# First modulations of a diffusion block: w_ada loaded and multiplied by eighths of the channels instead of quarters

## The chip, the cores and the metric

The kernel runs on one core of a Trainium2 chip. Its time is the device time of one execution in microseconds (us); three executions of the kernel before give a median of 2354.31 us (2351.40 to 2354.86). The engines are named as the profile names them: PE is TensorE (PEld its weight loads), DVE is VectorE, ACT is ScalarE, POOL is GpSimd, and SP issues DMAs (SPq, ACTq and POOLq are the engines' queues for it).

## The reference

One layer of a hybrid diffusion block. x and ctx are 256 tokens of 2048 channels each; everything is fp32.

```python
mod_c = jax.nn.silu(c_ctx) @ w_ada[l][:, :n_mod * D_MODEL] + b_ada[l][:n_mod * D_MODEL]   # n_mod = 2
mods_c = jnp.split(mod_c, n_mod)
... = _token_mixers(_modulate(h_ctx, mods_c[0], mods_c[1]), ...)      # context: states only
mod = jax.nn.silu(c) @ w_ada[l] + b_ada[l]
sh1, sc1, g1, sh2, sc2, g2 = [m[:, None, :] for m in jnp.split(mod, 6, axis=-1)]
y, _ = _token_mixers(_modulate(x, sh1, sc1), ...)                     # x * (1 + sc1) + sh1
x = _layernorm(ALPHA * x + g1 * y, ln1_g[l], ln1_b[l])
x = _layernorm(ALPHA * x + g2 * _sq_relu_mlp(_modulate(x, sh2, sc2), ...), ...)
```

Only the first two modulations (shift sh1 and scale sc1, for x from c and for ctx from c_ctx) concern the change: two vectors of 2048 inputs times the first 4096 columns of w_ada, 33.6 MB, then x and ctx scaled and shifted by them. The token mixers begin with projections u @ w_in; here the keys of the DeltaNet (512 columns) and its gates (32 columns, loaded as 128) stand at the opening.

## The kernel before

Channels are kept as 16 k-tiles of 128 (kt), tokens of x and ctx side by side as 512 columns. A fp32 product is made of three matmuls with operands split into a high and a low part (`split`: hi on ACT by line 138, lo on DVE by line 139); `cm_block` (lines 219 to 221) is such a triple.

The opening runs over quarters q of the channels (lines 368 to 393). For each quarter and each part (0 shift, 1 scale) `load_ada` asks for four raw tiles of w_ada, each 4 k-tiles by 512 columns (1 MB, 2 KB in a row); even calls go to a ring of two (`ring`), odd ones to general pages (`raw`, tag k8, seven buffers shared with xt and others). There are 32 such tiles. Line 380 multiplies a tile: four matmuls, one per k-tile, with the two silu'd conditioning vectors in 32 columns of weights (`cs32`), each into another 32 partitions of the PSUM bank `pmod`. When a part is complete, `mod_columns` copies the rows to SBUF (ACT, line 359), turns and sums them into columns by four small matmuls with `sel` (line 361), and adds the bias (DVE, lines 363 and 365). When shift and scale of a quarter are there, `modulated` transposes a k-tile of x and ctx on PE (line 171), applies scale and shift on ACT (line 352) and splits it into uh and ul. Then `keys` (two k-tiles, 24 matmuls of 512 columns into four banks psk) and `gates_in` (four k-tiles, 12 matmuls into the bank pga) use them. All these are put in the list `later` and taken from it between the tiles of the following quarter; what is left runs behind the last one. Two steps of the Hyena filters (`next(filt)`, line 255 and around) stand in it too.

Behind the opening come colB and colC (small tables: rows loaded by DMAs on ACT's queue into a tile that DVE cleared, line 181, then transposed on PE), the convolutions on the key banks (DVE, lines 521 to 525, cy), and the next projections over the context (`proj_cm_ctx`). Beside all projections run the loads `aw` of the other modulations' columns (line 540, 512 KB each) with a sum on DVE per load (lines 553 and 555); aw, the weights of projections and the gates' weights share four buffers of the tag wraw.

PSUM has eight banks: four of tag mm (at first psk) and four of tag ps (one is pga, three are left for pmod, transposes and filter steps). Within each engine the order of instructions is set when the program is built, by a scheduler that follows its own estimate of times; engines then run in that order and wait for each other by semaphores, and a DMA queue issues its DMAs in that order, each when its buffer is free.

Of the kernel before, what the change touches and what calls it, by code (L numbers as in the profile page):

```python
# [16 lines left out]
P = 128  # L17
D = 2048
# [62 lines left out]
def tile_block(ctx: ExitStack, tc: tile.TileContext, A: dict, out: bass.AP):  # L81
# [10 lines left out]
    def slot(shape, tag, name, dt=F32):  # L92
        uid[0] += 1
        return sbp.tile(shape, dt, name=f"{name}_{uid[0]}", tag=tag, bufs=NB[tag])
# [216 lines left out]
    uxh, uxl = uh[:, :, 0:T], ul[:, :, 0:T]  # L311
    uch, ucl = uh[:, :, T:], ul[:, :, T:]
    x_in, c_in = A["x"][0], A["ctx"][0]
    ring = slot([P, 2, 4, 512], "m16", "ring")
    turn = [0]

    def load_ada(k0, c0):

        n = turn[0]
        turn[0] += 1  # L320
        raw = ring[:, n // 2 % 2] if n % 2 == 0 else page("raw", (4, 512))
        nc.sync.dma_start(out=raw, in_=w_ada[k0 * P:(k0 + 4) * P, c0:c0 + 512].rearrange("(k p) c -> p k c", p=P))
        return raw

    psk = [mm_ps() for _ in range(4)]
# [16 lines left out]
                cm_block(psk[ch], wh, wl, ch, k, uh[:, kt, :], ul[:, kt, :], kt == 0, kt == KT - 1)  # L342

    def modulated(xt, mod, kt):
        cc = kt % 4
        pt = sc_ps()
        for i in range(4):
            transpose(pt[:, i * P:(i + 1) * P], xt[:, i, cc * P:(cc + 1) * P])
        uf = slot([P, 512], "k2", "uf")
        for i in range(2):  # L350
            sl = slice(i * T, (i + 1) * T)
            act(out=uf[:, sl], in_=pt[:, sl], func=AF.Identity, scale=mod[:, 1, cc, i:i + 1],
                bias=mod[:, 0, cc, i:i + 1])
        split(uf, uh[:, kt, :], ul[:, kt, :])

    def mod_columns(mod, part, pmod, q):

        row = slot([P, 512], "k2", "modrow")
        copy(out=row, in_=pmod)
        for cc in range(4):  # L360
            mm(pmod[:, 2 * cc:2 * cc + 2], row[:, cc * P:(cc + 1) * P], sel, start=True, stop=True)
        b = ba1[:, part * KT + 4 * q:part * KT + 4 * q + 4].unsqueeze(2)
        tt_(out=mod[:, part], in0=pmod[:, 0:8].rearrange("p (b c) -> p b c", b=4), in1=bc(b, [P, 4, 2]), op=ADD)
        if part == 1:
            ts_(out=mod[:, 1], in0=mod[:, 1], scalar1=1.0, scalar2=None, op0=ADD)

    later = []
    for q in range(4):
        xt = page("xt", (4, 512))
        for i, src in enumerate((x_in, c_in)):  # L370
            nc.scalar.dma_start(
                out=xt[:, 2 * i:2 * i + 2, :],
                in_=src[:, q * 512:(q + 1) * 512].rearrange("(t p) c -> p t c", p=P))
        mod = slot([P, 2, 4, 2], "k1", "mod")
        for part in range(2):
            pmod = sc_ps()
            for kb in range(4):
                raw = load_ada(4 * kb, part * D + q * 512)
                for j in range(4):
                    mm(pmod[32 * j:32 * j + 32, :], cs32[:, 4 * kb + j, :], raw[:, j, :],  # L380
                       start=(kb == 0), stop=(kb == 3))
                for _ in range(-(-len(later) // (8 - 4 * part - kb))):
                    later.pop(0)()
            if part == 0:
                mod_columns(mod, part, pmod, q)
        later.append(lambda mod=mod, pmod=pmod, q=q: mod_columns(mod, 1, pmod, q))
        for cc in range(4):
            later.append(lambda xt=xt, mod=mod, kt=4 * q + cc: modulated(xt, mod, kt))
        for kb in range(2):
            later.append(lambda k0=4 * q + 2 * kb: keys(k0))  # L390
        later.append(lambda k0=4 * q: gates_in(k0))
        if q in (1, 2):
            later.append(lambda: next(filt))
    for step in later:
        step()
# [1186 lines left out]
```

## Time and profile before

| | us |
|---|---|
| median of three executions | 2354.31 |
| the profiled execution | 2349.37 |
| its span, first to last instruction | 2347.7 |
| PE busy | 2242.3 (96%) |
| DVE busy | 1560.2 (66%) |
| ACT busy | 1022.2 (44%) |
| the 16 DMA engines, mean over the span | 218 GB/s |

The page of the profile gives the busy time of each engine over the span, and the same in 40 slices of 58.7 us. In the first slice PE is busy three tenths and DMA nine or more tenths at 361 GB/s; in the second PE is busy nine tenths and DMA again nine. From the third slice on PE is at nine tenths in all but the last. The chain of work that ended last is made of PE for 74% and of DMA for 11%. Matmul durations in the rows are the time of one instruction in a pipeline; what a stream of them takes is read from the distance between starts.

### The profile page before, as it was taken

The page shows a single profiled execution, that of the slowest core. Times are in us where ns is not written, and L with a number is a line of the kernel's source. Part 1 is how long each engine was busy: PE and PEld are TensorE (multiplying, and loading weights), DVE is VectorE, ACT ScalarE, POOL GpSimd, SP SyncE. Part 2 cuts the span into 40 slices and gives each one's busy share as a digit, 9 for nine tenths or more (in the row PEclk, how much of TensorE's full clock was granted, in tenths as well). Part 3 has the DMA queues.
Part 4 walks back from the last instruction along what each step waited for, and adds up shares of the span by engine and source line. Part 5 has one row for each costly group of instructions (what it writes and reads, how often), then busy time and mean ns, then how long its engine had stood idle before and what let it go on. Part 6 is the DMA issues. An engine that isn't in the chain of part 4 may idle for free.

```text
span 2347.7 us, 32567 instructions
## 1 busy us (share of the span) xinstructions
PE 2242.3 (96%) x12641; PEld 1892.4 (81%) x12641; DVE 1560.2 (66%) x1910; ACT 1022.2 (44%) x1410; POOL 182.1 (8%) x293
## 2 busy tenths in 40 slices
PE   3989999999999999999999999999999999999998
PEld 1558789889888989887888877887888888888886
DVE  1256467877889998676666656666765766765667
ACT  2345534434432533644443433444544544544542
POOL 0000221000200000111120021000000000000000
PEclk8989999999999999999999999999999999999999
DMA  9957867777653323678787888664677777776664
GB/s 361 355 164 231 252 186 230 239 255 251 198 152 100 95 82 112 181 205 279 232 250 219 293 319 275 217 217 143 208 230 243 233 244 247 229 247 190 197 203 147
DMA packets 296135, 511.19 MB, mean 218 GB/s; under 512 B 17590, under 2 KB 155281, under 8 KB 293388
## 3 DMA queue, kind: packets, MB, share of 16 engines
q1 hardware_dynamic: 271552, 422.63, 56.1%
q0 software_dynamic: 21648, 82.01, 11.3%
q10 hardware_dynamic: 2780, 4.47, 0.5%
q8 instruction: 99, 1.62, 0.3%
q14 instruction: 56, 0.46, 0.1%
HBM read 474.59 MB, written 34.45 MB: 217 GB/s over the span
## 4 chain that ended last, share of the span: by engine, by line
PE 74%; DMA 11%; DVE 7%; issue 5%; ACT 2%; POOL 1%; ACTq 0%; DVEq 0%; POOLq 0%; SPq 0%
PE mm L467 10%; PE mm L510 7%; PE mm L511 7%; PE mm L509 7%; DMA aw<-in_w_ada_dram 5%; PE mm L469 5%; PE mm L219 4%; PE mm L220 4%; PE mm L221 4%; PE mm L837 3%; PE mm L838 3%; PE mm L836 3%; DVE wlo L139 2%; DMA wraw<-in_w_branch_dram 2%; PE ps L380 1%
## 5 line engine op out<-in xcount | busy, mean ns | idle before, releaser
L138 ACT CAST whi<-wraw 128x1024 fp32r<-128x1024 f32 x592 | 622.2, 1052 | 898.2 <-PE mm L511 221.8
L139 DVE TENSOR_TENSOR wlo<-wraw,whi 128x1024 fp32r<-128x1024 f32 x592 | 721.6, 1221 | 413.4 <-PE mm L510 129.9
L467 PE MATMUL mm<-u,whi 128*128 128x512 f32 x992 | 350.6, 399 | 0.0
L219 PE MATMUL mm<-uh,whi 128*128 128x256 f32 (+1 forms) x1024 | 340.1, 336 | 8.9 <-DVE cy L525 6.3
L221 PE MATMUL mm<-uh,wlo 128*128 128x256 f32 (+1 forms) x1024 | 342.0, 335 | 2.5 <-DVE wlo L139 2.5
L220 PE MATMUL mm<-ul,whi 128*128 128x256 f32 (+1 forms) x1024 | 342.5, 334 | 0.0
L469 PE MATMUL mm<-u,wlo 128*128 128x256 f32 x992 | 278.6, 281 | 0.0
L467 PEld LDWEIGHTS mm<-u,whi 128*128 128x128 f32 x992 | 186.4, 188 | 46.5
L219 PEld LDWEIGHTS mm<-uh,whi 128*128 128x128 f32 x1024 | 197.4, 193 | 32.5 <-issue 6.0
L221 PEld LDWEIGHTS mm<-uh,wlo 128*128 128x128 f32 x1024 | 197.3, 193 | 23.0 <-DVE wlo L139 3.5
L220 PEld LDWEIGHTS mm<-ul,whi 128*128 128x128 f32 x1024 | 197.2, 193 | 20.3 <-issue 2.7
L469 PEld LDWEIGHTS mm<-u,wlo 128*128 128x128 f32 x992 | 187.4, 189 | 0.1
L511 PE MATMUL mm<-whi,h 128*128 128x512 f32 x480 | 187.2, 390 | 0.0
L510 PE MATMUL mm<-wlo,h 128*128 128x512 f32 x480 | 186.8, 389 | 0.0
L509 PE MATMUL mm<-whi,h 128*128 128x512 f32 x480 | 186.0, 391 | 0.0
L555 DVE SCALAR_TENSOR_TENSOR acc<-aw,csil,acc 128x1024 f32<-128x1024 f32 x90 | 115.4, 1282 | 104.1 <-DMA aw<-in_w_ada_dram 103.8
L837 PE MATMUL mm<-wlo,uh 128*128 128x512 f32 x384 | 150.8, 393 | 2.2 <-DVE wlo L139 2.2
L838 PE MATMUL mm<-whi,ul 128*128 128x512 f32 x384 | 151.2, 394 | 0.0
L836 PE MATMUL mm<-whi,uh 128*128 128x512 f32 x384 | 151.1, 400 | 0.0
L509 PEld LDWEIGHTS mm<-whi,h 128*128 128x128 f32 x480 | 90.1, 188 | 19.4 <-issue 0.7
L510 PEld LDWEIGHTS mm<-wlo,h 128*128 128x128 f32 x480 | 90.1, 188 | 19.1 <-issue 0.5
L511 PEld LDWEIGHTS mm<-whi,h 128*128 128x128 f32 x480 | 90.1, 188 | 19.0 <-issue 0.2
(509 smaller groups left out, 3640.3 us busy)
## 6 DMA issues: line engine op xcount, KB each, us to landing
wraw<-in_w_in_dram SPq DMA_DIRECT2D x272, 512.0 KB, 4.5
wraw<-in_w_ff_dram SPq DMA_DIRECT2D x256, 512.0 KB, 4.0
aw<-in_w_ada_dram SPq DMA_DIRECT2D x96, 512.0 KB, 4.3
wraw<-in_w_branch_dram SPq DMA_DIRECT2D x48, 512.0 KB, 5.7
ring<-in_w_ada_dram SPq DMA_DIRECT2D x16, 1024.0 KB, 9.2
raw<-in_w_ada_dram SPq DMA_DIRECT2D x16, 1024.0 KB, 12.0
wraw<-in_w_out_dram SPq DMA_DIRECT2D x32, 512.0 KB, 4.5
awr<-in_w_ada_dram SPq DMA_DIRECT2D x32, 512.0 KB, 5.1
```

What stands on the lines that cost most here:

```text
L138: copy(out=hi, in_=src)
L139: tt_(out=lo, in0=src, in1=hi.bitcast(F32), op=SUB)
L219: mm(ps, wh[:, k, cs], ah, start=first, stop=False, skip_group_check=True)
L220: mm(ps, wh[:, k, cs], al, start=False, stop=False, skip_group_check=True)
L221: mm(ps, wl[:, k, cs], ah, start=False, stop=last, skip_group_check=True)
L467: mm(pss[ch], wh[:, k, cs], a[:, kt].rearrange("p s t -> p (s t)"), start=(kt == 0), stop=False, skip_group_check=True)
L469: mm(pss[ch][:, 0:T], wl[:, k, cs], a[:, kt, 0], start=False, stop=(kt == KT - 1), skip_group_check=True)
L509: mm(pss[i], a, wh[:, k, :], start=(kt == 0), stop=False)
L510: mm(pss[i], a, wl[:, k, :], start=False, stop=False)
L511: mm(pss[i], b, wh[:, k, :], start=False, stop=(kt == nk - 1))
L836: mm(pg[i], a, wh[:, k, :], start=(kt == 0), stop=False)
L838: mm(pg[i], c, wh[:, k, :], start=False, stop=(kt == KT - 1))
```

## The change

The loop runs over eighths q of the channels, 256 columns each. A raw tile is 8 k-tiles by 256 columns: the same 1 MB, in rows of 1 KB. There are again 32 of them, two for the shift and two for the scale of an eighth. Each is multiplied by eight matmuls of 256 columns, k-tile k into the 32 partitions of k modulo 4, so that two matmuls of a tile follow each other in the same partitions. Shift and scale of an eighth lie in one PSUM bank, 256 columns each, and `mod_columns` handles both at once: one copy of 512 columns, four small matmuls, one bias add for both, and the addition of 1 to the scale. It runs eight times, as before, but always in `later`, where before the shift's ran directly. An eighth has two k-tiles to modulate, one `keys`, and after every second eighth one `gates_in`. xt is still loaded 512 columns at a time, on even q.

```diff
-    ring = slot([P, 2, 4, 512], "m16", "ring")
+    ring = slot([P, 2, 8, 256], "m16", "ring")
...
-        raw = ring[:, n // 2 % 2] if n % 2 == 0 else page("raw", (4, 512))
-        nc.sync.dma_start(out=raw, in_=w_ada[k0 * P:(k0 + 4) * P, c0:c0 + 512].rearrange("(k p) c -> p k c", p=P))
+        raw = ring[:, n // 2 % 2] if n % 2 == 0 else page("raw", (8, 256))
+        nc.sync.dma_start(out=raw, in_=w_ada[k0 * P:(k0 + 8) * P, c0:c0 + 256].rearrange("(k p) c -> p k c", p=P))
...
-    def mod_columns(mod, part, pmod, q):
+    def mod_columns(mod, pmod, q):
...
-        for cc in range(4):
-            mm(pmod[:, 2 * cc:2 * cc + 2], row[:, cc * P:(cc + 1) * P], sel, start=True, stop=True)
-        b = ba1[:, part * KT + 4 * q:part * KT + 4 * q + 4].unsqueeze(2)
-        tt_(out=mod[:, part], in0=pmod[:, 0:8].rearrange("p (b c) -> p b c", b=4), in1=bc(b, [P, 4, 2]), op=ADD)
-        if part == 1:
-            ts_(out=mod[:, 1], in0=mod[:, 1], scalar1=1.0, scalar2=None, op0=ADD)
+        for c in range(4):
+            mm(pmod[:, 2 * c:2 * c + 2], row[:, c * P:(c + 1) * P], sel, start=True, stop=True)
+        b = ba1.rearrange("p (a k) -> p a k", a=2)[:, :, 2 * q:2 * q + 2].unsqueeze(3)
+        tt_(out=mod, in0=pmod[:, 0:8].rearrange("p (a b c) -> p a b c", a=2, b=2), in1=bc(b, [P, 2, 2, 2]), op=ADD)
+        ts_(out=mod[:, 1], in0=mod[:, 1], scalar1=1.0, scalar2=None, op0=ADD)
...
-    for q in range(4):
-        xt = page("xt", (4, 512))
+    for q in range(8):
+        if q % 2 == 0:
+            xt = page("xt", (4, 512))
...
-        mod = slot([P, 2, 4, 2], "k1", "mod")
+        mod = slot([P, 2, 2, 2], "k1", "mod")
+        pmod = sc_ps()
         for part in range(2):
-            pmod = sc_ps()
-            for kb in range(4):
-                raw = load_ada(4 * kb, part * D + q * 512)
-                for j in range(4):
-                    mm(pmod[32 * j:32 * j + 32, :], cs32[:, 4 * kb + j, :], raw[:, j, :],
-                       start=(kb == 0), stop=(kb == 3))
-                for _ in range(-(-len(later) // (8 - 4 * part - kb))):
+            for kb in range(2):
+                raw = load_ada(8 * kb, part * D + q * 256)
+                for k in range(8):
+                    j, n = k % 4, 2 * kb + k // 4
+                    mm(pmod[32 * j:32 * j + 32, part * 256:(part + 1) * 256], cs32[:, 8 * kb + k, :], raw[:, k, :],
+                       start=(n == 0), stop=(n == 3))
+                for _ in range(-(-len(later) // (4 - 2 * part - kb))):
                     later.pop(0)()
-            if part == 0:
-                mod_columns(mod, part, pmod, q)
-        later.append(lambda mod=mod, pmod=pmod, q=q: mod_columns(mod, 1, pmod, q))
-        for cc in range(4):
-            later.append(lambda xt=xt, mod=mod, kt=4 * q + cc: modulated(xt, mod, kt))
-        for kb in range(2):
-            later.append(lambda k0=4 * q + 2 * kb: keys(k0))
-        later.append(lambda k0=4 * q: gates_in(k0))
-        if q in (1, 2):
+        later.append(lambda mod=mod, pmod=pmod, q=q: mod_columns(mod, pmod, q))
+        for cc in range(2):
+            later.append(lambda xt=xt, mod=mod, kt=2 * q + cc: modulated(xt, mod, kt))
+        later.append(lambda k0=2 * q: keys(k0))
+        if q % 2:
+            later.append(lambda k0=2 * q - 2: gates_in(k0))
+        if q in (3, 5):
             later.append(lambda: next(filt))
```

How the built order moves is shown at three places. First PE between tile 5 and the first keys; ps_140 and ps_167 are banks pmod, xt_106 the first tile of x and ctx, mm_101 to mm_104 the key banks. Before:

```order
L380 MATMUL ps_140<-ring_100,cs_3_80 32x512 x4
L380 MATMUL ps_140<-raw_146,cs_3_80 32x512 x4
L380 MATMUL ps_140<-ring_100,cs_3_80 32x512 x4
L380 MATMUL ps_140<-raw_157,cs_3_80 32x512 x4
L361 MATMUL ps_140<-sel,modrow_173 128x2 x4
L380 MATMUL ps_167<-ring_100,cs_3_80 32x512 x4
L380 MATMUL ps_167<-raw_181,cs_3_80 32x512 x4
L171 MATMUL ps_187<-idon,xt_106 128x128 x4
L171 MATMUL ps_202<-idon,xt_106 128x128 x4
L171 MATMUL ps_218<-idon,xt_106 128x128 x4
L380 MATMUL ps_167<-ring_100,cs_3_80 32x512 x4
L380 MATMUL ps_167<-raw_212,cs_3_80 32x512 x4
```

Here tiles 5 to 12 stand ahead of the first key matmul, which is the next row. The same place after (line 381 is now the tiles' line):

```order
L381 MATMUL ps_150<-ring_100,cs_3_80 32x256 x8
L381 MATMUL ps_150<-raw_168,cs_3_80 32x256 x8
L171 MATMUL ps_178<-idon,xt_106 128x128 x4
L171 MATMUL ps_197<-idon,xt_106 128x128 x4
L381 MATMUL ps_150<-ring_100,cs_3_80 32x256 x8
L381 MATMUL ps_150<-raw_207,cs_3_80 32x256 x8
L219 MATMUL mm_101<-uh_98,whi_219 128x512
L219 MATMUL mm_102<-uh_98,whi_219 128x512
L219 MATMUL mm_103<-uh_98,whi_219 128x512
L219 MATMUL mm_104<-uh_98,whi_219 128x512
```

The first keys have moved from behind tile 12 to behind tile 8. The second place is PE at the last tiles, from the end of the third gate block (ps_105 is the gates' bank pga). Before:

```order
L219 MATMUL ps_105<-uh_98,wg_710 128x512
L220 MATMUL ps_105<-ul_99,wg_710 128x512
L221 MATMUL ps_105<-uh_98,wg_711 128x512
L380 MATMUL ps_632<-raw_727,cs_3_80 32x512 x4
L255 MATMUL ps_733<-z_540,w_77_533 64x256
L171 MATMUL ps_753<-idon,xt_550 128x128 x4
L171 MATMUL ps_763<-idon,xt_550 128x128 x4
L361 MATMUL ps_632<-sel,modrow_745 128x2 x4
L171 MATMUL ps_773<-idon,xt_550 128x128 x4
L171 MATMUL ps_783<-idon,xt_550 128x128 x4
L171 MATMUL ps_882<-idon,colB_rows_876 128x128
L171 MATMUL ps_893<-idon,colC_rows_885 128x128
```

After, from the same gate block's last matmuls:

```order
L220 MATMUL ps_105<-ul_99,wg_794 128x512
L221 MATMUL ps_105<-uh_98,wg_795 128x512
L381 MATMUL ps_706<-raw_811,cs_3_80 32x256 x8
L381 MATMUL ps_834<-ring_100,cs_3_80 32x256 x8
L381 MATMUL ps_834<-raw_852,cs_3_80 32x256 x8
L171 MATMUL ps_862<-idon,xt_702 128x128 x4
L361 MATMUL ps_706<-sel,modrow_844 128x2 x4
L381 MATMUL ps_834<-ring_100,cs_3_80 32x256 x8
L381 MATMUL ps_834<-raw_891,cs_3_80 32x256 x8
L171 MATMUL ps_881<-idon,xt_702 128x128 x4
L171 MATMUL ps_939<-idon,xt_702 128x128 x4
L219 MATMUL mm_101<-uh_98,whi_903 128x512
```

Before, only tile 32 stands behind that gate block, and all 48 last key matmuls stand behind colB and colC. After, tiles 28 to 32 stand behind it; the keys of the seventh eighth (whi_903) follow, and colB's transpose stands between them and the last 24 keys. The third place is DVE at the last eighth's modulation (mod_833; acc_1303 is the sum of the aw loads, wlo_1312 the low part of a later projection's weights). After:

```order
L552 TENSOR_SCALAR acc_1303<-aw_1304,csil 128x1024
L139 TENSOR_TENSOR ul_99<-uf_867,uh_98 128x512
L554 SCALAR_TENSOR_TENSOR acc_1303<-aw_1306,csil,acc_1303 128x1024
L139 TENSOR_TENSOR ul_99<-uf_886,uh_98 128x512
L139 TENSOR_TENSOR wlo_1312<-wraw_1309,whi_1311 128x1024
L554 SCALAR_TENSOR_TENSOR acc_1303<-aw_1339,csil,acc_1303 128x1024
L363 TENSOR_TENSOR mod_833<-ps_834,colA 128x8
L181 MEMSET colB_rows_1012 128x128
L181 MEMSET colC_rows_1021 128x128
```

Before, the last part's modulation there (mod_553 from the bank ps_632):

```order
L181 MEMSET colC_rows_885 128x128
L258 TENSOR_SCALAR z_736<-z_735 64x256
L259 TENSOR_SCALAR z_736<-z_736 64x256
L553 TENSOR_SCALAR acc_1167<-aw_1168,csil 128x1024
L261 SCALAR_TENSOR_TENSOR z_735<-z_736,z_735 64x256
L363 TENSOR_TENSOR mod_553<-ps_632,colA 128x8
```

One sum of aw stood ahead of the last modulation, now three and a weight split do; the two memsets stood ahead of it and now stand behind it.

## Rows read from the trace of the kernel before

**Rows 1.** Timeline of PE: start, us, instruction, [idle before, releaser]; 24 to 62 us
```profile
24.15 1.93 PE L380 MATMUL ps<-ring,cs 128*32 128x512 f32 x8 [11.68 <-DVE cs L205]
...
38.68 1.94 PE L380 MATMUL ps<-ring,cs 128*32 128x512 f32 x8 [6.91 <-DMA ring<-in_w_ada_dram]
...
44.10 1.07 PE L380 MATMUL ps<-ring,cs 128*32 128x512 f32 x8 [1.78 <-DMA ring<-in_w_ada_dram]
44.98 1.04 PE L380 MATMUL ps<-raw,cs 128*32 128x512 f32 x8
...
58.67 1.29 PE L380 MATMUL ps<-ring,cs 128*32 128x512 f32 x8 [2.20 <-DMA ring<-in_w_ada_dram]
...
61.60 1.72 PE L219 MATMUL mm<-uh,whi 128*128 128x512 f32 x4
```

**Rows 2.** Stretches: us, busy PE PEld DVE ACT POOL, granted clock, DMA share, GB/s
```profile
24.15:61.60 37.45, 22.49 (x125) 7.57 (x125) 3.63 (x7) 7.65 (x13) 0.00 (x0) 0.74 1.05 384
61.60:136.55 74.95, 73.82 (x423) 45.83 (x420) 18.34 (x34) 22.18 (x40) 2.16 (x4) 0.99 0.81 287
```

**Rows 3.** Stretches: DMA at rest, and DMA with rows of 1 KB (w_ff1)
```profile
66.00:71.00 5.00, 5.00 (x35) 3.29 (x37) 1.30 (x2) 0.77 (x2) 0.00 (x0) 1.00 0.45 168
...
1599.50:1602.00 2.50, 2.50 (x13) 2.07 (x12) 2.19 (x4) 1.23 (x2) 0.00 (x0) 1.00 1.08 362
```

**Rows 4.** DMA packets of 28 to 36 us (2 KB) and of 1597 to 1602 us (1 KB)
```profile
DMA packets 1574, 3.09 MB, mean 387 GB/s; under 512 B 64, under 2 KB 64, under 8 KB 1574
...
DMA packets 1454, 1.46 MB, mean 291 GB/s; under 512 B 33, under 2 KB 1454, under 8 KB 1454
```

**Rows 5.** Timeline of PE and its weight loads: prices of tiles, products and matmuls
```profile
30.71 0.97 PEld L361 LDWEIGHTS ps<-sel,modrow 128*128 128x128 f32 x8 [1.62 <-ACT modrow L359]
...
88.00 1.06 PE L380 MATMUL ps<-ring,cs 128*32 128x512 f32 x8
...
88.45 0.13 PEld L380 LDWEIGHTS ps<-raw,cs 128*32 128x32 f32 x4 [0.30 <-issue]
...
88.88 1.04 PE L380 MATMUL ps<-raw,cs 128*32 128x512 f32 x8
...
92.18 0.39 PE L221 MATMUL mm<-uh,wlo 128*128 128x512 f32 x1
92.41 0.39 PE L220 MATMUL mm<-ul,whi 128*128 128x512 f32 x1
...
173.07 0.28 PE L220 MATMUL mm<-ul,whi 128*128 128x256 f32 x1
173.19 0.28 PE L221 MATMUL mm<-uh,wlo 128*128 128x256 f32 x1
```

**Rows 6.** Timeline of PE: third gate block's last matmul, first matmul of the next projection
```profile
135.16 0.40 PE L221 MATMUL ps<-uh,wg 128*128 128x512 f32 x1
...
169.02 0.58 PE L219 MATMUL mm<-uh,whi 128*128 128x256 f32 x1 [4.67 <-DVE cy L525]
```

**Rows 7.** Chain that ended last: start, us, what; a transpose set, a filter step
```profile
70.23 0.59 PE ps L171 x4
...
136.55 0.59 PE ps L255 x2
```

**Rows 8.** Timeline of DVE, 139 to 164 us: sums of aw, first convolution step
```profile
139.54 0.75 DVE L553 TENSOR_SCALAR acc<-aw,csil 128x1024 f32<-128x1024 f32 x1 [1.26 <-DMA aw<-in_w_ada_dram]
...
162.13 1.28 DVE L555 SCALAR_TENSOR_TENSOR acc<-aw,csil,acc 128x1024 f32<-128x1024 f32 x1 [4.84 <-DMA aw<-in_w_ada_dram]
163.33 0.86 DVE L521 SCALAR_TENSOR_TENSOR cy<-mm,colC,cy 128x252 f32<-128x252 f32 x2
```

**Rows 9.** Chain that ended last: DMAs in it, issue to landing
```profile
139.16 2.11 DMA colC_rows<-in_dn_conv_k_dram
...
157.32 4.72 DMA aw<-in_w_ada_dram
```

**Rows 10.** Stretch from the first projection behind the opening to the end
```profile
169.00:2347.70 2178.70, 2124.69 (x12006) 1822.67 (x12006) 1513.70 (x1815) 971.31 (x1325) 175.82 (x278) 0.99 0.67 212
```

More of the change, by code (lines that the diff above doesn't have):

```diff
@@ L344, in modulated @@
     def modulated(xt, mod, kt):
-        cc = kt % 4
+        xs, cc = slice((kt % 4) * P, (kt % 4 + 1) * P), kt % 2
         pt = sc_ps()
         for i in range(4):
-            transpose(pt[:, i * P:(i + 1) * P], xt[:, i, cc * P:(cc + 1) * P])
+            transpose(pt[:, i * P:(i + 1) * P], xt[:, i, xs])
         uf = slot([P, 512], "k2", "uf")
@@ L367, in tile_block @@
-    later = []
-    for q in range(4):
-        xt = page("xt", (4, 512))
[L370 to L373, printed above, removed]
-        mod = slot([P, 2, 4, 2], "k1", "mod")
-        for part in range(2):
-            pmod = sc_ps()
-            for kb in range(4):
-                raw = load_ada(4 * kb, part * D + q * 512)
-                for j in range(4):
-                    mm(pmod[32 * j:32 * j + 32, :], cs32[:, 4 * kb + j, :], raw[:, j, :],
-                       start=(kb == 0), stop=(kb == 3))
-                for _ in range(-(-len(later) // (8 - 4 * part - kb))):
-                    later.pop(0)()
-            if part == 0:
-                mod_columns(mod, part, pmod, q)
-        later.append(lambda mod=mod, pmod=pmod, q=q: mod_columns(mod, 1, pmod, q))
-        for cc in range(4):
-            later.append(lambda xt=xt, mod=mod, kt=4 * q + cc: modulated(xt, mod, kt))
-        for kb in range(2):
-            later.append(lambda k0=4 * q + 2 * kb: keys(k0))
-        later.append(lambda k0=4 * q: gates_in(k0))
-        if q in (1, 2):
@@ new lines, in mod_columns @@
+        for c in range(4):
[3 more added lines that the diff above has]
+        ts_(out=mod[:, 1], in0=mod[:, 1], scalar1=1.0, scalar2=None, op0=ADD)
+    later = []
+    for q in range(8):
+        if q % 2 == 0:
+            xt = page("xt", (4, 512))
+            for i, src in enumerate((x_in, c_in)):
+                nc.scalar.dma_start(
+                    out=xt[:, 2 * i:2 * i + 2, :],
+                    in_=src[:, q * 256:(q + 2) * 256].rearrange("(t p) c -> p t c", p=P))
+        mod = slot([P, 2, 2, 2], "k1", "mod")
+        pmod = sc_ps()
+        for part in range(2):
+            for kb in range(2):
[5 more added lines that the diff above has]
+                for _ in range(-(-len(later) // (4 - 2 * part - kb))):
+                    later.pop(0)()
+        later.append(lambda mod=mod, pmod=pmod, q=q: mod_columns(mod, pmod, q))
[5 more added lines that the diff above has]
+        if q in (3, 5):
```

## The prediction

> **What bounds the kernel now.** I read the busy shares first (TensorE, called PE below, 96% of the span), then tables of busy time by stretch, then PE's own instructions in order of time, then the chain that ended last, and last the DMA and VectorE rows at the places where PE waits. Tiles of w_ada are numbered 1 to 32 in the order in which they are asked for; odd ones lie in the ring, even ones in pages.
>
> Over most of the kernel PE is the bound: from 169.0 us to the end it is busy 2124.7 of 2178.7 us [rows 10]. The change touches only the opening. There PE starts on tile 1 at 24.15 us, waits 6.9 us for tile 5, 1.8 us for tile 7, 2.2 us for tile 11, and begins the first key projection at 61.60 us, behind tile 12 [rows 1]. In 24.15 to 61.60 it is busy 22.5 of 37.5 us at a mean granted clock of 0.74 while the DMA engines are full (384 GB/s); from 61.60 to 136.55 it is busy 73.8 of 75.0 us at 0.99 and the DMA engines have slack (287 GB/s) [rows 2]. DMA is at rest for most of 66 to 71 us [rows 3]. So the opening has two halves: first DMA is the bound and PE idles for want of a finished modulation, then PE is the bound and works off keys that it could have begun earlier.
>
> **The change, part by part.**
> *Earlier keys.* Before, the shift and scale of 4 k-tiles are complete after 8 tiles, and the order puts tiles 9 to 12 ahead of the first keys. After, those of 2 k-tiles are complete after 4 tiles, and in PE's order the first 24 key matmuls stand right behind tile 8. Tile 7 runs at 44.10 us and tile 8 at 44.98 us, 0.9 us each [rows 1], so at an unchanged DMA rate the keys could start at about 46.0. The rows of a tile in memory shrink from 2 KB to 1 KB, and the DMA rate with them: rows of 2 KB ran at 387 GB/s in a full stretch, rows of 1 KB at 362 GB/s in the one full stretch of them that I found [rows 3, 4]. About 9.5 MB of tiles are moved by then: 9.5/0.362 - 9.5/0.387 = 1.7 us more. Keys start at about 47.7 instead of 61.6: **-13.9 us**.
>
> [...]
>
> *PE work from there to the third gate block.* Take as mark the last matmul of the third of the four gate blocks: before it starts at 135.16 and ends at 135.5 us [rows 6]. Between the first key and this mark PE does 12 k-tiles of keys, 12 of gates, 19 tiles and 5 sets of column products, before and after alike (before tiles 13 to 31, after tiles 9 to 27). After has one transpose set more (0.59 us) and the second filter step (0.59 us) [rows 7]: **+1.2 us**.
>
> *The tiles themselves.* A tile has 8 matmuls of 256 columns where it had 4 of 512, and in the trace each is two passes. Four column groups run side by side, so the streamed columns are the same; two tiles in a row start 0.88 us apart, and the weight loads of a pass (0.13 us for four) begin when the pass before has ended and lie under the running pass of 0.44 us [rows 5]. With half the columns a pass is about 0.22 us and still covers 0.13. What remains is the fixed part of a pass. In the projections matmuls of 512 columns start every 0.23 us and those of 256 every 0.12 [rows 5], so 2 x 0.12 - 0.227 = 0.013 us does not halve; a tile has two passes more, 0.03 us, and 19 x 0.03 = **+0.6 us**. The bounds: nothing, if the parts overlap fully; and if each weight load with its matmul took what the loads of 128 columns take, 0.97/8 = 0.12 us [rows 5], a tile would take 1.9 us, 19 us in all. I take the low end, since eight narrow loads fit in a fraction of a microsecond there.
>
> [...]
>
> *Short waits.* Column products come per eighth, each with a copy on ScalarE and two VectorE steps ahead of the activations; in the packed stretch before, all of PE's idle time is 75.0 - 73.8 = 1.1 us [rows 2] for five sets. I add **+1 us** (0 to 3). The mark moves from 135.5 to 135.5 - 13.9 + 1.2 + 0.6 + 1.0 = 124.4 us.
>
> *Does DMA keep up?* Before tile 31 has landed 43.4 MB must come: 33.6 of w_ada, 4.2 of x and ctx, 4.2 of key weights, 1.4 of the rest. At 0.362 for the first and 0.387 MB/us for the others that is 92.7 + 25.3 = 118 us, from about 3.5 us: 121.5. PE wants tile 31 about 4.4 us after the mark, at 128.8. There are 7 us of slack, more than the rest at 66 to 71 us cost [rows 3]; so no term.
>
> *The tail.* Before, from the mark to the first matmul of the next projection (169.02) are 33.5 us [rows 6]. Tiles 28 to 32 now stand behind the mark where only tile 32 did: 4 x 0.9 = 3.6 us more, and one set of column products; but only half of the last keys depend on the last tile. Were that all, PE would run through: some 60 matmuls at 0.227 us [rows 5], 5 tiles, 4 transpose sets, 2 sets of column products, 23 us; from the first step of the convolution to the projection it was 5.7 us [rows 6, 8] and an activation or two stand ahead, say 7: 30 us, -3.5. Against it stands VectorE's order. The aw loads of the later modulation have two buffers free until the gates are done, and VectorE adds them up in order: it waited 1.3 us for one at 139.5 and 4.8 us at 162.1, and the convolution began behind that at 163.3 [rows 8]. After, three of these sums and a weight split stand ahead of the last eighth's modulation. PE has that ready at about mark + 12.2 (5 tiles 4.5, transposes 2.4, column products 1.9, 15 matmuls 3.4). VectorE gets to it later: the first aw lands 4.7 us after its issue [rows 9] and behind tile 31 (1.05 MB, 2.9 us), its sum frees the buffer (0.8), the next load takes 4.7, a split and a sum about 1.3 each: mark + 15.7. Behind it wait, in this order, the memset of colB_rows, three small DMAs on ScalarE's queue among four activations (3.5 us together, by the durations of such steps, and 2.1 until the last lands [rows 9]), and colB's transpose on PE, which now stands ahead of the last two k-tiles of keys. PE has run out at mark + 15.6 and stands still until about mark + 21.5, finishes 30 matmuls at mark + 29 to 30, the two buffers turn once more ahead of the convolution (mark + 33.5), and the first projection starts at about mark + 37.4, 3.9 us later than before. So -3.5 to +3.9 us; I take **+2**, nearer to the waiting end since before showed those very waits.
>
> *Sum.* -13.9 + 1.2 + 0.6 + 1.0 + 2.0 = **-9.1 us**: the first projection at 160 instead of 169. Behind it nothing is changed but the order of single instructions up to some 520 us; PE is busy 97.5% there [rows 10], so the shift stays, plus or minus 3 us. The profiled execution took 2349.4 us (span 2347.7 and 1.7 around it), 4.9 us under the median of the three runs; it would become 2340.3, and the median of 2354.3 becomes **2345.2 us**.
>
> **The rivals.**
> *The tail eats it.* The mark at 127 (waits of 3 us and more in the packed stretch), the tail at its worst, and reordering against us: -8.5 + 3.9 + 1 is about -3.5, 2350.8. For it: VectorE's waits for aw held the convolution already before [rows 8]. Against: the keys of the seventh eighth now fill PE while the last modulation is formed.
> *Slower: 1 KB rows.* If 33.6 MB of 1 KB rows run no faster than 291 GB/s, the mean of the only stretch that had nothing else, ramp included [rows 4], w_ada alone takes 115 us, tile 31 lands at 3.5 + 25.3 + 115 = 144, and the first projection comes 31 us behind that, at 175: +6 us, 2360. The place is the DMA engines in 30 to 140 us; it decides below some 308 GB/s, where the landing is 138. Against it: 362 GB/s once the queues were full.
> *More gain.* If VectorE and ScalarE never hold PE up, the tail is -3.5 and the sum -14.6: 2339.7.
> *The change does not do what it says.* The order rules it out: the first keys stand behind tile 8.
>
> **How the numbers follow.** Forecast 0.54, tail eats it 0.24, more gain 0.10, 1 KB rows or slow tiles 0.12. About 0.2% (4.7 us) can be told from no change. The forecast's own spread is 2342 to 2350, nearly all of it faster; with the gain case and a sliver of the second, faster has 0.65, within 0.2% 0.24, slower 0.11. For 8 in 10 the range takes in the gain case at its edge and the second rival with room for reordering: 2339 to 2355.
>
> **What would show it.** In the profile after: the first key matmul near 48 us; two tiles in a row 0.9 us apart; w_ada at about 360 GB/s; the mark near 124; VectorE waiting for aw, and PE for colB, near 140 to 147 us; the first projection near 160; the rest shifted by the same 9 us. It is wrong if tiles take over 1.2 us, if DMA falls under 310 GB/s, or if later stretches do not keep the shift.

## The result: slower by 0.6%

The change made the kernel slower. Four executions of each on one chip: 2365.91 us (median) after, 2352.91 before, ratio 1.006 with an interval of 1.0048 to 1.0072. I had forecast 2345.2. The profiled execution of after took 2366.49 us, of which 2364.8 are its span; that of before 2349.37 and 2347.7.

First PE of the changed kernel in order of time: start, duration, instruction, and in brackets the idle time before it with what ended it. These rows answer to [rows 1, 5, 6].

```profile
25.71 1.93 PE L381 MATMUL ps<-ring,cs 128*32 128x256 f32 x16 [11.59 <-DVE cs L205]
...
42.37 1.93 PE L381 MATMUL ps<-ring,cs 128*32 128x256 f32 x16 [9.01 <-DMA ring<-in_w_ada_dram]
...
48.38 1.07 PE L381 MATMUL ps<-ring,cs 128*32 128x256 f32 x16 [0.69 <-DMA ring<-in_w_ada_dram]
...
50.24 1.20 PE L219 MATMUL mm<-uh,whi 128*128 128x512 f32 x4
...
76.10 1.07 PE L381 MATMUL ps<-ring,cs 128*32 128x256 f32 x16 [1.08 <-DMA ring<-in_w_ada_dram]
76.99 1.05 PE L381 MATMUL ps<-raw,cs 128*32 128x256 f32 x16
...
131.67 0.40 PE L221 MATMUL ps<-uh,wg 128*128 128x512 f32 x1
...
136.99 1.05 PE L381 MATMUL ps<-raw,cs 128*32 128x256 f32 x16
...
152.16 0.45 PE L171 MATMUL ps<-idon,colB_rows 128*128 128x128 f32 x1 [4.90 <-DMA colB_rows<-in_dn_conv_v_dram]
...
168.40 0.58 PE L219 MATMUL mm<-uh,whi 128*128 128x256 f32 x1 [2.59 <-DVE cy L524]
...
260.48 1.94 PE L171 MATMUL ps<-idon,qtok 128*128 128x128 f32 x8 [5.29 <-DVE qtok L595]
...
448.60 0.40 PE L235 MATMUL ps<-hv,dcon 128*128 128x512 f32 x1
```

The last row, the first matmul with hv and dcon (the Hyena branch and its Fourier matrices), is a landmark that I use from here on: it comes 12.5 us later than in the kernel before (436.08). The last tile of w_ada and the landmark in the kernel before:

```profile
135.49 1.06 PE L380 MATMUL ps<-raw,cs 128*32 128x512 f32 x8
...
436.08 0.40 PE L235 MATMUL ps<-hv,dcon 128*128 128x512 f32 x1
```

Milestones of the two executions, in us:

| | before | after | moved |
|---|---|---|---|
| first key matmul | 61.60 | 50.24 | -11.4 |
| end of the third gate block (the mark) | 135.56 | 132.07 | -3.5 |
| first projection | 169.02 | 168.40 | -0.6 |
| first matmul hv, dcon (the landmark) | 436.08 | 448.60 | +12.5 |
| end of the span | 2347.7 | 2364.8 | +17.1 |

Tables of busy time by stretch, columns as in [rows 2]. The changed kernel, the first two stretches to be read beside [rows 2], the others beside the table below them:

```profile
25.71:50.24 24.53, 14.12 (x144) 7.45 (x144) 2.23 (x5) 5.64 (x9) 0.00 (x0) 0.72 1.09 351
50.24:131.90 81.66, 75.73 (x572) 51.34 (x568) 21.83 (x45) 24.96 (x44) 2.18 (x4) 0.98 0.99 322
50.24:97.20 46.96, 41.56 (x323) 27.94 (x319) 9.89 (x18) 14.47 (x25) 1.61 (x3) 0.98 1.09 353
168.40:448.60 280.20, 258.07 (x1623) 230.99 (x1624) 173.79 (x276) 136.98 (x237) 49.72 (x78) 0.96 0.71 219
448.60:2364.80 1916.20, 1873.45 (x10386) 1596.32 (x10384) 1341.24 (x1548) 840.19 (x1091) 125.68 (x200) 0.99 0.66 209
```

The kernel before, from its first projection to the landmark and from there to the end:

```profile
169.02:436.10 267.08, 255.06 (x1623) 229.19 (x1624) 173.55 (x268) 133.08 (x234) 49.92 (x78) 0.97 0.73 224
436.10:2347.70 1911.60, 1869.63 (x10386) 1593.47 (x10384) 1340.13 (x1548) 838.21 (x1091) 125.90 (x200) 0.99 0.66 210
```

Between first projection and landmark both kernels make the same 1623 matmuls, but the stretch takes 280.2 us instead of 267.1: 22.1 us of it idle on PE instead of 12.0, and 3 us more busy. So there were two questions: why the opening gave 0.6 us and not 9.1, and why a stretch that the diff does not touch got 13 us longer.

### The profile page after: what moved, and what is told of

Its sections match the earlier page's. It is cut to its first block, busy times and chain, and to the rows that moved or that the text cites. A ratio compares the mean times of both kernels' runs of the same rounds, so it can differ in the third digit from the quotient of the medians.

```text
span 2364.8 us, 33089 instructions
## 1 busy us (share of the span) xinstructions
PE 2246.9 (95%) x12897; PEld 1905.3 (81%) x12897; DVE 1561.3 (66%) x1914; ACT 1028.8 (44%) x1412; POOL 181.7 (8%) x293
## 4 chain that ended last, share of the span: by engine, by line
PE 68%; DMA 7%; DVE 5%; issue 2%; ACT 1%; POOL 0%; DVEq 0%; ACTq 0%; POOLq 0%; SPq 0%
PE mm L466 10%; PE mm L509 7%; PE mm L510 7%; PE mm L508 7%; PE mm L468 5%; DMA aw<-in_w_ada_dram 4%; PE mm L836 4%; PE mm L837 4%; PE mm L835 4%; PE mm L220 3%; PE mm L221 3%; PE mm L219 3%; DVE wlo L139 2%; DMA wraw<-in_w_in_dram 1%; PE mm L970 1%
```

## Experiments

**Opening and order, crossed.** Theory A: the other order of the instructions behind the opening makes the loss. Theory B: the opening makes it, and later stages hand it on. What stands behind the opening in the program is the same in both kernels; only its order on each engine differs. The built orders of the two differ at 250 of 1847 places on DVE, 157 of 1262 on ACT, 861 of 11250 on PE and 8 of 284 on POOL, and at none on SP, whose queue asks for its loads behind the opening in the same order. So I held that order: a list of places, taken from the other kernel as built, and an edge of order (no wait) between each instruction and the next one of its engine. How these instructions stand among those of the opening stays free.

```diff
+    opening = {i.name for i in nc.cur_bb.bb.instructions}
...
+    rest = [i for i in nc.cur_bb.bb.instructions if i.name not in opening]
+    for engine, packed in ORDER.items():
+        mine = [i for i in rest if str(i.engine).split(".")[-1] == engine]
+        at = np.cumsum(np.frombuffer(zlib.decompress(base64.b85decode(packed)), "<i2").astype(int))
+        for one, two in zip(at, at[1:]):
+            tc.add_manual_dep(
+                mine[two], mine[one].name,
+                mybir.DependencyInfo(mybir.DependencyClass.NoSync, mybir.DependencyReason.DATA), reason="order")
```

Names in what follows: *gates* are DVE's steps that form the DeltaNet's gates, *G* is their result, *ktok* and *qtok* are the keys and queries turned to rows of tokens, *dfts* the Fourier matrices of the Hyena filters. A sum "ahead of" one of them stands before it in DVE's order.

The eighths with the order of the kernel before:

> The changed opening (eighths), but every instruction that stands behind the opening in the program is held, engine by engine, in the order that it has in the kernel before. Theory A (the loss is made by the other order behind the opening): the first projection starts near 168, as with the change, the stretch from there to the end is 2179 us as before and not 2196, and the time is 2350 to 2354 us. Theory B (the loss follows from the opening itself: slower rows of 1 KB and a last eighth that comes late, which a later stage hands on): the time stays near 2366 us, at least 2361, whatever the order.

The quarters with the order of the changed kernel:

> The opening of the kernel before (quarters), but everything behind it held in the order that it has in the changed kernel. Theory A (order): 2366 us or more, 13 us over before, with PE idle ahead of the transposes of qtok and of the filters' dfts as in the changed kernel. Theory B (the opening): within 3 us of before, 2350 to 2356.

Measured: eighths in the old order 1.0025 of before (1.0012 to 1.0037), quarters in the new order 1.0058 (1.0036 to 1.0081). The quarters' opening is the old one, and yet they take the whole loss of the change (1.006). The same stretch, from first projection to landmark, first of the quarters in the new order, then of the eighths in the old one:

```profile
177.26:456.30 279.04, 255.88 (x1623) 229.53 (x1624) 174.06 (x276) 136.67 (x237) 49.74 (x78) 0.96 0.70 216
```

```profile
173.60:434.60 261.00, 251.05 (x1623) 225.71 (x1624) 173.48 (x268) 131.89 (x231) 49.82 (x78) 0.99 0.73 226
```

Theory A holds for the larger part: 279 and 280 us in the new order, 261 and 267 in the old, whichever opening stands ahead. But theory A expected the first projection near 168 and a time of 2350 to 2354 with the old order. It was 2355.28, still 0.25% over before, and the first projection came at 173.60. PE's rows of the eighths in the old order:

```profile
169.21 0.63 PE L618 MATMUL ps<-idon,gT 32*128 32x32 f32 x4 [12.96 <-ACT gT L615]
...
173.60 0.58 PE L219 MATMUL mm<-uh,whi 128*128 128x256 f32 x1 [3.76 <-DVE cy L525]
```

Keys and gates were done at 156, four us earlier than in the kernel before, and PE then stood still for 13 us; its row names ACT (gT) as what ended that, and within it DVE waited 0.84 and 3.34 us for loads of aw. And still the landmark came at 434.56, earlier than before (436.08): the time of the first projection was not what set it.

**1 KB rows by themselves.** Quarters, old order, but raw tiles of 8 k-tiles by 256 columns:

```diff
+                h, k0 = kb // 2, kb % 2 * 8
+                raw = load_ada(k0, part * D + q * 512 + h * 256)
+                for k in range(8):
+                    j, n = k % 4, (k0 + k) // 4
+                    mm(pmod[32 * j:32 * j + 32, h * 256:(h + 1) * 256], cs32[:, k0 + k, :], raw[:, k, :],
+                       start=(n == 0), stop=(n == 3))
```

> Quarters as before and everything behind the opening in the old order, but each raw tile is 8 k-tiles by 256 columns, rows of 1 KB, eight matmuls of 256 columns a tile. Only row size and matmul width change. Theory C (1 KB rows cost the opening its gain): DMA runs at about 350 GB/s instead of 384 while PE waits for tiles, the first keys start 3 to 4 us later than 61.6, and the time is 3 to 8 us over before, 2356 to 2361. Rival (row size is hidden by the slack that DMA had from 62 us on): first keys 3 us later, but the first projection within 1 us of 169.0 and the time within 2 us of before.

Measured 1.0033 (1.0020 to 1.0046), 7.8 us by the ratio: theory C, though the first keys came 4.9 us later (66.5 instead of 61.6) and not 3 to 4. From the first tile to the first keys its table of stretches has

```profile
25.39:66.50 41.11, 22.77 (x221) 11.25 (x221) 3.62 (x7) 7.64 (x13) 0.00 (x0) 0.73 1.09 352
```

352 GB/s where [rows 2] has 384, at a full DMA share in both (1.09 and 1.05). The last tile is multiplied 8 us later than before (143.5), so it was not hidden. The sizes of 4.9 and 8 us are those of single executions: in the other four kernels with the quarters' opening and rows of 2 KB (new order, or aw delayed) the first keys came at 63.3 to 63.6 and the last tile at 136.7 to 139.7.

**The aw loads out of the tail.** In the kernel before, the chain that ended last runs through the loads of aw between 147 and 250 us. Four of its pieces (start, us, what):

```profile
148.56 6.28 DMA aw<-in_w_ada_dram
...
181.28 5.04 DMA aw<-in_w_ada_dram
...
231.62 9.16 DMA aw<-in_w_ada_dram
...
242.11 6.76 DMA aw<-in_w_ada_dram
```

Theory D: this loop (load, sum on DVE, buffer free, next load) bounds the stretch. Edit, for both openings: aw begins eight weight loads later.

```diff
     beside("ada", ada_parts(range(6)), 1.0)
+    side["ada"][2] = -8.0
...
-    go_on("ada", 0.55)
+    go_on("ada", 0.67)
```

Quarters:

> The kernel before, but the aw loads of the later modulation and their sums on DVE begin eight weight loads later (their rate further on is raised from 0.55 to 0.67, so that all 96 still come in time). In the kernel before, DVE waits 1.3, 3.8 and 4.8 us for aw between 139 and 162 us, and the first convolution step stands behind that at 163.3. Theory D (the loop aw load, sum, buffer free, next load bounds 140 to 250 us): the last gates end some 2 to 4 us before 160.0, the first projection starts at 160 to 165 instead of 169.0, and the time is 4 to 10 us under before. Rival (what is saved there is waited for later, by the same number of loads): first projection earlier, but the time within 3 us of before.

Eighths:

> The changed kernel with the same delay of the aw loads and sums. Theory D: with the aw loop out of the way the last gates end at about 152 to 156 us instead of 161.2, the first projection starts at 158 to 162 as I had forecast for the change, and the time falls from 2366 to 2340 to 2350. Rival (the order behind the opening, not aw, costs the 13 us): first projection near 160, G still behind 200, time over 2355.

Eighths, held in the order that these quarters have:

> Eighths with the delayed aw, and everything behind the opening in the order that the quarters with delayed aw have. Against quarters with delayed aw only the opening differs. If earlier keys are worth what I forecast once nothing stands in the tail, this is 5 to 10 us under quarters with delayed aw, with the first projection 5 to 9 us earlier. Rival (1 KB rows and the later stages take it): within 2 us of it, or slower.

Quarters, held in the order that these eighths have:

> Quarters with the aw loads eight weight loads later, and everything behind the opening held in the order that the eighths with delayed aw have (2341 us, 0.995 of before). Theory E (only the order behind the opening decides, and in it how many aw sums stand on DVE ahead of gates, G and qtok): within 4 us of that, 0.993 to 0.997 of before. Theory F (the eighths' earlier keys are what gains, once no aw stands in the tail): the first projection some 6 us later than 163, and the time 6 to 10 us over the eighths', near 1.000.

Measured: quarters 1.0006 (0.9993 to 1.0019), eighths 0.9952 (0.9938 to 0.9966), eighths in the quarters' order 1.0028 (1.0013 to 1.0043), quarters in the eighths' order 0.9954 (0.9935 to 0.9973). Taken alone, the first two look like the forecast gain of earlier keys once the tail is free. The crossed pair takes that away: the quarters have the same gain in the same order. First projection to landmark, of the eighths and of the quarters in that order:

```profile
163.00:424.70 261.70, 255.29 (x1624) 230.20 (x1624) 175.25 (x278) 131.97 (x236) 49.47 (x78) 0.96 0.74 230
```

```profile
168.80:424.10 255.30, 249.52 (x1623) 225.27 (x1623) 174.61 (x278) 131.68 (x236) 49.51 (x78) 0.99 0.75 235
```

The eighths' first projection is 5.8 us earlier, the landmark 0.6 us later. Eighths with aw delayed are some 11 us faster than the kernel before, but not by their opening. Theory D by itself also falls for the quarters in their own order: first projection at 164, as expected, and no gain, as its rival said. The last gates did not end early as it expected: at 163.1 in the quarters (not ahead of 160) and at 158.5 in the eighths (not at 152 to 156).

A longer delay (16 weight loads, rate 0.78) was to show whether fewer aw sums ahead are better still:

> The kernel before with the aw loads sixteen weight loads later (later rate 0.78); on DVE no aw sum then stands ahead of gates, G or ktok and three ahead of qtok, where the kernel before has 5, 12, 18 and 21. Theory E: without sums that wait for DMA ahead of these steps, G comes at 182 to 188 instead of 198 and qtok at 232 to 240 instead of 252, and the time is 8 to 14 us under before. Rival (what is put off is paid between 440 and 700 us, where the eighths with delayed aw lost 9 us): under 4 us of gain.

> The changed kernel with the aw loads sixteen weight loads later; none ahead of gates, G and ktok, two ahead of qtok. Theory E: as quarters with the same delay, within 3 us, both 8 to 14 us under before. Theory F: 5 to 8 us under those quarters.

Measured 0.9958 (0.9944 to 0.9972) and 0.9966 (0.9949 to 0.9983): no difference between the openings, the landmark at 428.8 and 420.8. In the eighths part of the 15.3 us gained by then is given back behind it (8 us are left by the ratio); for the quarters (7.3 us by then, 9.9 by the ratio) it is not shown. That agrees with theory E as far as the openings go.

**Where on which engine.** Only DVE's order held as before:

```diff
-    for engine, packed in ORDER.items():
+    for engine, packed in [("DVE", ORDER["DVE"])]:
```

> The changed kernel; of what stands behind the opening only DVE's instructions are held in the order of the kernel before, the other engines' are left to the scheduler. On DVE then 5, 12, 18 and 21 aw sums stand ahead of gates, G, ktok and qtok again, where the changed kernel has 7, 14, 19 and 22. If DVE's order (these sums above all) makes the loss: the time is that of the eighths with the whole old order, 1.0015 to 1.0035 of before, G near 203 and dfts near 287. If it lies in the order of PE or ACT: it stays near 1.006.

Measured 1.0013 (1.0002 to 1.0024), landmark at 435.88: holding DVE's order is enough to undo most of the loss. It does not show that the loss lies on DVE, because the scheduler plans the other engines anew around the held one. In the changed kernel as built, the pairs of instructions that stand the other way round than in the kernel before are 493 on DVE, 6931 on PE and 165 on ACT; in this run they are 0, 791 and 33. PE and ACT are nearly back in the old order too.

I took the loss for DVE's and the aw sums for its cause, since 7, 14, 19 and 22 of them stand on DVE ahead of gates, G, ktok and qtok, where it was 5, 12, 18 and 21 (counted in DVE's rows). At qtok one sees such a sum hold up PE. DVE's rows, the kernel before and then the changed one:

```profile
248.96 1.28 DVE L555 SCALAR_TENSOR_TENSOR acc<-aw,csil,acc 128x1024 f32<-128x1024 f32 x1 [6.88 <-DMA aw<-in_w_ada_dram]
```

```profile
257.27 1.28 DVE L554 SCALAR_TENSOR_TENSOR acc<-aw,csil,acc 128x1024 f32<-128x1024 f32 x1 [9.11 <-DMA aw<-in_w_ada_dram]
...
260.05 1.66 DVE L595 TENSOR_SCALAR qtok<-qtok,ss_q 128x128 f32<-128x128 f32 x8
```

Edit: the changed kernel with DVE's order held; in it only the sums move, from the sixth on the k-th to the place of the (k+2)-th. The other engines are left to the scheduler.

> The changed kernel with DVE's order behind the opening held as it is there, except that of the aw sums the sixth to the 26th stand two places of such sums later: 5, 12, 17 and 20 of them ahead of gates, G, ktok and qtok instead of 7, 14, 19 and 22. If sums that wait for aw loads are what the new order costs: G near 198 to 200 instead of 204, qtok at 252 to 256 instead of 260, and the time 1.000 to 1.003 of before. If it is the other steps' places on DVE: it stays at 1.005 to 1.007.

Measured 1.0081 (1.0061 to 1.0102), qtok at 266.6 instead of 252 to 256: slower still, and what my explanation foretold did not come. What DVE and ACT waited for between 140 and 320 us (in all, times, longest), of this run and then of the changed kernel:

```profile
DVE acc L555 <- DMA aw<-in_w_ada_dram: 17.8, 4, 7.0
...
ACT whi L138 <- DMA wraw<-in_w_in_dram: 44.5, 12, 8.6
```

```profile
DVE acc L554 <- DMA aw<-in_w_ada_dram: 46.4, 16, 9.1
...
ACT whi L138 <- DMA wraw<-in_w_in_dram: 16.7, 6, 4.9
```

DVE's wait for aw did fall, from 46.4 to 17.8 us (34.9 in the kernel before). But a sum that comes later frees its wraw buffer later, and the projections' weights take turns in the same four: ACT's wait for them rose from 16.7 to 44.5. The wait changed engines. PE's order was planned anew here as well (2237 pairs turned against the changed kernel), so the run does not price the sums by themselves.

Then DVE's order in two halves, divided behind the copies into G: the first 75 places of the old list, and the other 1772.

> The changed kernel; on DVE only the first 75 instructions behind the opening (to the copies into G) are held in the order of the kernel before, all else is left to the scheduler. If the loss lies there (the opening's tail and the gates): 1.000 to 1.003 of before, as with DVE's whole old order, and dfts at 286 to 290. If it lies behind G: 1.005 or more, dfts near 296.

> The other half: DVE's instructions behind the copies into G are held in the old order among themselves, the 75 ahead of them are left to the scheduler (7 and 13 aw sums ahead of gates and G, 18 and 21 ahead of ktok and qtok). If the loss lies ahead of G: 1.005 to 1.007, G near 204 and dfts near 296. If it lies behind G: 1.000 to 1.003, G near 204 but dfts at 286 to 290.

Measured 0.9980 (0.9961 to 1.0000) and 1.0001 (0.9984 to 1.0018). Either half undoes the loss; both have the landmark back at 436.1 and 435.1. But a held half draws the rest after it: of the 493 turned pairs on DVE and 6931 on PE, 69 and 1855 are left with the first half held, 203 and 2708 with the second. So the halves do not divide the loss, and which steps make it, on which engine, is left open. What is shown is that the order on all engines together makes it.

**Early keys without 1 KB rows.** Only the first quarter by eighths, the other 24 tiles as before:

```diff
+    for q in range(2):
...
+                raw = load_ada(8 * kb, 8, part * D + q * 256, 256)
...
+    for q in range(1, 4):
...
+                raw = load_ada(4 * kb, 4, part * D + q * 512, 512)
```

> Only the first quarter is taken by eighths (eight tiles of 1 KB rows, keys begin behind tile 8); the other 24 tiles are 512 columns wide with rows of 2 KB, as before. aw is not delayed; on DVE 5, 10, 16 and 19 sums stand ahead of gates, G, ktok and qtok. If 1 KB rows cost the change its gain up to the third gate block: first keys near 49, the mark (last matmul of the third gate block) at 126 to 128 instead of 132, and the tail no later than in the kernel before; time 2 to 8 us under before. If what is gained there is waited for in the tail (the aw loop) anyway: first projection within 3 us of 169 and the time within 4 us of before.

Measured 0.9963 (0.9948 to 0.9979), 8.7 us of gain by the ratio where 2 to 8 were expected, and not for the reason given: the first keys came at 49.2, but the mark at 139.4 (expected 126 to 128), the last tile at 139 and the first projection at 174.2. PE's waits from the first keys to the mark:

```profile
PE ps L413 <- DMA ring<-in_w_ada_dram: 5.2, 3, 3.4
PE ps L171 <- DVE mod L374: 4.3, 1, 4.3
```

Line 413 multiplies the tiles with rows of 2 KB. So behind early keys PE waits for tiles with these rows too. The landmark stood at 435.8, as before; behind it this execution took 1907.7 us instead of 1911.6, less than executions differ there, so where the gain arises is not shown. With aw delayed as well, in the order of the eighths and then in its own:

> Only the first quarter by eighths (rows of 2 KB from the second quarter on), aw eight weight loads later, and everything behind the opening in the order of the eighths with delayed aw. In that order the quarters measured 0.9954 of before and the eighths 0.9952. Theory E (the order decides, the opening is worth nothing): 0.994 to 0.997. If early keys without the price of 1 KB rows are worth something there: 0.990 to 0.993.

> Only the first quarter by eighths, aw eight weight loads later, the order behind the opening left to the scheduler: 0, 5, 11 and 14 aw sums ahead of gates, G, ktok and qtok. If the held order did not fit this opening (in it the tail stood until 171 where the eighths' stood until 163): first projection at 160 to 166 and 0.992 to 0.997. If this opening has nothing to give beside delayed aw: 0.998 to 1.001 like the quarters in their own order (1.0006, with the same counts).

Measured 0.9998 (0.9986 to 1.0010) and 1.0005 (0.9990 to 1.0020). The second is what was expected of an opening with nothing to give. The first lies outside every expectation: the held order that had given 0.995 behind two openings gave nothing behind the third, whose first projection came at 171.1 (163.0 and 168.8 with the others) and whose landmark at 432.8. Why is open; an order that suits one opening need not suit another.

The crossed runs in one table (us in the profiled execution; the ratio is to the kernel before on the same chip):

| opening | order behind | first keys | first projection | landmark | ratio |
|---|---|---|---|---|---|
| quarters | old (before) | 61.6 | 169.0 | 436.1 | 1 |
| eighths | old | 49.9 | 173.6 | 434.6 | 1.0025 |
| quarters, 1 KB rows | old | 66.5 | 176.5 | 438.8 | 1.0033 |
| eighths | new (after) | 50.2 | 168.4 | 448.6 | 1.006 |
| quarters | new | 63.3 | 177.3 | 456.3 | 1.0058 |
| quarters, aw later | own | 63.4 | 164.1 | 435.5 | 1.0006 |
| eighths, aw later | that of the quarters | 49.9 | 166.1 | 439.0 | 1.0028 |
| eighths, aw later | own | 50.0 | 163.0 | 424.7 | 0.9952 |
| quarters, aw later | that of the eighths | 63.6 | 168.8 | 424.1 | 0.9954 |

In four pairs only the opening differs. The eighths against the quarters: +0.25%, 0, +0.2%, 0. The third opening, the first quarter by eighths, is a fifth case: in the order of the eighths with aw later it is 0.45% slower than either. So the price of an opening and that of an order do not simply add up. Where only the order differs, it is 0.35% (eighths) and 0.6% (quarters) between new and old, 0.5 and 0.8% between the two orders with aw later.

## Why the prediction was wrong

**First keys** (forecast 47.7, measured 50.24). Direction right, the size of one term wrong. I charged 1 KB rows with 1.7 us from 362 GB/s, read in a stretch of 2.5 us. Over 25.71 to 50.24 they ran at 351, against 384 before, and the keys came 4.2 us behind the 46.0 of an unchanged rate. With these two rates the 9.5 MB make 2.3 us; the other 1.9 us were not in the term. Tile 1 itself started 1.6 us later (25.71 instead of 24.15); whether that is the rest is not shown. Between the two sizes these stretches show 9.4% (384/351), where the ones I had read differ by 6.9% (387/362).

**Tiles** (+0.03 us each). Right: two in a row start 0.89 us apart (76.10, 76.99), against 0.88 before [rows 5].

**From first keys to the mark** (forecast 124.4, measured 132.07). This is the step of the opening that failed: "There are 7 us of slack, ... so no term". From first key to the mark it took 81.8 us, where [rows 1, 6] give 73.9 for before. PE's busy time grew by some 3 us (75.7 against the 73.8 of [rows 2] less the 1.0 behind the mark; I had 1.8), its idle time from 1.1 to 5.9. PE's waits in the packed stretch of the changed kernel:

```profile
PE ps L381 <- DMA ring<-in_w_ada_dram: 5.4, 3, 2.7
```

I had checked the DMA's total against the last tile only. In between, from 50.24 to 97.20, the queues were full at 353 GB/s (DMA share 1.09), and PE, which starts the keys earlier, reaches tiles that have not come. Earlier keys moved work from behind the stream of w_ada into its time. From 97.20 on PE waited for no tile any more; the last one starts at 136.99 behind PE's own work, before at 135.49, so the early start was used up. With rows of 2 KB behind the first quarter the same waits came to 5.2 us, so the row size alone does not make them.

**The tail** (+2, between -3.5 and +3.9). Right, though the +2 was chosen between two worked cases: from the mark to the first projection 36.3 us instead of 33.5, so +2.9, and with the stall that I named: PE waits for colB from 147.26 to 152.16, 15.2 to 20.1 us behind the mark (forecast 15.6 to 21.5).

**The sum at the first projection** is therefore -0.6 instead of -9.1: 2.5 us less at the first keys, 1.3 more work, 3.8 more idle, 0.9 more in the tail, which makes 8.5.

**"Behind it nothing is changed but the order of single instructions ... so the shift stays, plus or minus 3 us."** This failed by 17.7 us in the profiled executions, and it is the step that turned the sign. Of these, 13.1 lie ahead of the landmark, and the crossed runs show them to be the order's. The other 4.6 are not more than such executions differ there: from the landmark to the end of the span it is 1907.4 us in the quarters with the new order and 1919.5 in the eighths with aw later, which are the faster kernel. Nor can one count on a shift to stay: in the old order 7.5 us at the first projection (169.0 to 176.5) left the landmark within 4.3 us, in the new one 8.9 us became 7.7, and in that of the eighths with aw later 5.8 us became -0.6. I had taken the stretch for PE's, because PE was busy for 97.5% of the time behind 169 us [rows 10]; that is a mean over 2179 us. The chain had DMA of aw in it up to 250 us, and I used it only for the tail.

**The rivals.** Slower was among them, but as one mechanism, rows of 1 KB at 291 GB/s. They do cost 0.33% when nothing else changes but the width of the tiles' matmuls, at 352 GB/s; the larger part of what happened had no rival of its own. The order had been seen to differ up to some 520 us, and it was worth a rival with a price of 10 us and more on both sides.

## What to carry to other kernels

Where a scheduler sets the order, an edit changes two things, its own work and the order of all that comes behind; hold the order of the rest, on all engines, to price them apart (here 0 to 0.25% and 0.35 to 0.8%). Holding one engine is another change: the scheduler plans the others anew around it. And do not credit the edit with a gain before the old version has run in the new order. An earlier start lasted here only up to the next stream that was full (11.4 us at the first keys, 3.5 at the mark): compare it with the arrival of every tile on the way, not of the last one. And what a later stretch hands on is read from the chain in that stretch, not from a busy share over the whole span.

A version faster than both kernels came out of it: eighths with aw eight weight loads later, 0.9952 of before; quarters in that order are as good at 0.9954.

## What the runs showed of the hardware

Rows of 1 KB against 2 KB with the queues full: 351 to 353 GB/s against 384, over 25 to 47 us, a larger gap than the short stretches of the trace before had shown (362 against 387). From the first tile to the first keys it is 384 in the kernel before, 351 in the changed one and 352 in the quarters with rows of 1 KB.

Behind some stalls PE ran at half the granted clock for a few us. In the changed kernel it idled for 5.29 us ahead of the transposes of qtok; before that the clock was 1.00 (245.00 to 255.20). Behind the transposes the matmuls of 512 columns start every 0.43 us at a granted clock of 0.50, and then every 0.23 us at 1.00. Rows of the changed kernel's PE timeline, and its table of both stretches:

```profile
262.64 0.63 PE L219 MATMUL mm<-uh,whi 128*128 128x512 f32 x1
263.07 0.63 PE L220 MATMUL mm<-ul,whi 128*128 128x512 f32 x1
...
265.63 0.47 PE L220 MATMUL mm<-ul,whi 128*128 128x512 f32 x1
...
266.17 0.39 PE L219 MATMUL mm<-uh,whi 128*128 128x512 f32 x1
266.40 0.39 PE L220 MATMUL mm<-ul,whi 128*128 128x512 f32 x1
```

```profile
262.64:265.63 2.99, 2.99 (x8) 2.32 (x7) 1.41 (x3) 1.35 (x2) 2.29 (x4) 0.50 0.56 138
...
266.17:269.00 2.83, 2.83 (x17) 2.43 (x15) 0.67 (x1) 0.00 (x0) 0.00 (x0) 1.00 0.99 361
```

From 262.64 to 265.63 seven matmuls take 3.0 us where seven at 0.23 take 1.6. The kernel before idles for 2.72 us ahead of its qtok and has matmuls every 0.43 us at 0.50 behind it too (254.61 to 257.17); behind 2.96 us of idle time ahead of ktok the changed kernel stayed at 1.00 (232.67 to 242.00). From the first projection to the landmark the two kernels differ by 10 us of idle time and by 3 us of busy time for the same matmuls; two such stretches more would make the latter, but that they do is not shown.
